# A state-space recurrence issued in another order beside its projections, and small transfers joined

## The chip, the cores and the metric

The kernel runs on one core of one Trainium2 chip. The metric is the device time of one execution in microseconds (us), and lower is better. The engines of the core are TensorE (PE: matmuls; PEld: its weight loads), VectorE (DVE), ScalarE (ACT), GpSimd (POOL) and SyncE (SP). In this kernel every transfer (DMA) is issued on SP.

## The reference

One step of a two-layer decoder trunk of width 1,024, for a prompt of 2,048 tokens and for 8 samples of one token each. The first layer has an RG-LRU and a gated DeltaNet of 8 heads side by side; the second is a complex diagonal state-space model (S5) with 64 groups of 16 channels and 64 complex states per group; a final RMSNorm follows. The second layer, cut to what matters:

```python
def s5_mixer(h, ...):
    u, z = jnp.split(jnp.dot(h, in_w), 2, axis=-1)
    ...
    Bu = einsum("gpc,blgc->lbgp", B_bar, u)
    Bu[0] += A_bar * x0                     # the given state, zero for the prompt
    xs = associative_scan(x[t] = A_bar * x[t-1] + Bu[t])
    y = einsum("gcp,lbgp->blgc", C, xs).real + d * u
    y = gelu(y)
    y = y * sigmoid(y @ glu_w + glu_b)      # the GLU
    y = y * silu(z)                         # the gate path
    return y @ out_w, xs[-1].real, xs[-1].imag
```

## The kernel before, in words

The prompt is worked in two halves of 1,024 tokens; in half 0 the 8 samples ride along as 8 more columns (1,032). Every projection is done in units: 128 output channels by all columns, 8 blocks of the contraction dimension (k = 0 to 7), and three matmuls each, because operands are split into a high and a low part (`in_unit`, L865, its matmul at L876). A unit's results leave PSUM by an `evac` function.

**Background work.** The recurrences run beside the units as generators in lanes (class `Fibers`, L35). After each `BURST` = 1,536 columns of projection matmuls, `pump` lets each lane go on by one step, that is to its next `yield`; `wait(n)` is n steps. `drain` runs a lane to its end with no projection matmul between. A scheduler with priorities then sets each engine's final order, and each engine runs its queue in that order; so the order rows below are read, and not the code's order alone.

**Second layer, per half** (loop at L1838). The first product of the layer gives u (8 units) and z (8 units). For i = 0 to 9 the loop does u-unit i and then z-unit i − 2, so the order is u0 u1 u2 z0 u3 z1 ... u7 z5 z6 z7. After u-unit i its result goes through DRAM (`dU`) into a transposed tile `uc`, the block's lane (`s50` for even i, `s51` for odd) is drained, and the block's generator `s5` is added to it. A z-unit leaves SiLU(z) in `sz`, and one unit later GpSimd multiplies it by the block's result `yg` (L1876). After the loop both lanes are drained, all 8 `yg` are split into high and low parts, and 8 GLU units and 8 output units follow.

**A block, `s5`** (L1702): 128 channels, 8 groups, in two quads of four groups, one after the other. It waits 9 steps and loads a table `MT`. A quad loads its tables `RT`, `ct`, `st`, waits 6 steps, and does four matmuls with `RT` (L1729); VectorE multiplies and adds (`s5t`), 4 steps later (6 in half 0) does four scans, and multiplies and adds again; 14 steps after the scans four pairs of matmuls with `MT` and `O` follow (L1786, L1787), and ScalarE puts the GELU back into `uc`. In half 0 a quad also carries the samples: matmuls at L1740, a transpose at L1749, `s5xa` on VectorE, matmuls at L1776 (`s5uo`), two more steps of waiting. At a block's end `uc` goes through DRAM (`dY`) into `yg`.

**Other parts that the change touches.** Weights come by a `Stream` (L242) that is one unit ahead; in half 0 of a layer ScalarE and GpSimd split them (`wlo`, L234). `final0` (L1815) is the final norm of half 0, 8 blocks: load `xf`, multiply on VectorE (L1834), store; it runs in lane `fn` during half 1's recurrence, every second step. In the first layer `gdn_prep` inverts triangular 16 x 16 blocks of a head: matrix `AT` (L964) goes to DRAM in 8 pieces (`fsd`) and comes back as `fsA` (F), VectorE solves in 15 steps (L1001), the results go to DRAM (`fst`) and come back in 16 pieces as `zt`, `zo` and `U32`, which the DeltaNet's matmuls read (L1053).

Of the kernel before, what the change touches and what calls it, by code (L numbers as in the profile page):

```python
# [2071 lines left out]
```

## Time and profile before

| | |
|---|---|
| time, median of 3 runs | 3163.17 us (3158.49 to 3163.83) |
| the profiled execution's own time | 3162.53 us |
| its span (first to last instruction) | 3160.6 us |
| mean granted TensorE clock | 0.967 of full speed |
| busy: PE, PEld, DVE, ACT, POOL | 2946.8, 2577.6, 2077.0, 1109.6, 689.1 us |
| DMA | 51.0% of 16 engines' time, 404,136 packets, 532.09 MB |
| chain of waits, by engine | PE 57%, DVE 26%, DMA 7%, issue 4% |

A window's row gives the stretch in us from the span's start, its length, and for PE, PEld, DVE, ACT and POOL the busy us (and instructions); then the granted TensorE clock (1.00 is 2.4 GHz, 0.50 is 1.2 GHz), the DMA share and GB/s. The stages are: 100 to 930 the first half of the first layer, 930 to 1170 the end of it with the output projection, 1170 to 2003 its second half; in the second layer 2215 to 2520 the recurrence of half 0, 2520 to 2610 its GLU, 2712 to 2960 the recurrence of half 1, and 3050 to 3160 the last output projection with the final norm. A waits row names the instruction that waited, by engine, tile and line, and what ended the wait. In a timeline row the bracket is the engine's idle time just before, with its releaser. L127 and L115 are helpers that record many VectorE instructions and all DMAs; there the tiles' names tell them apart.

### The profile page before, as it was taken

The page shows a single profiled execution, that of the slowest core. Times are in us where ns is not written, and L with a number is a line of the kernel's source. Part 1 is how long each engine was busy: PE and PEld are TensorE (multiplying, and loading weights), DVE is VectorE, ACT ScalarE, POOL GpSimd, SP SyncE. Part 2 cuts the span into 40 slices and gives each one's busy share as a digit, 9 for nine tenths or more (in the row PEclk, how much of TensorE's full clock was granted, in tenths as well). Part 3 has the DMA queues.
Part 4 walks back from the last instruction along what each step waited for, and adds up shares of the span by engine and source line. Part 5 has one row for each costly group of instructions (what it writes and reads, how often), then busy time and mean ns, then how long its engine had stood idle before and what let it go on. Part 6 is the DMA issues. An engine that isn't in the chain of part 4 may idle for free.

```text
span 3160.6 us, 54048 instructions
## 1 busy us (share of the span) xinstructions
PE 2946.8 (93%) x19958; PEld 2577.6 (82%) x19958; DVE 2077.0 (66%) x5468; ACT 1109.6 (35%) x2023; POOL 689.1 (22%) x672
## 2 busy tenths in 40 slices
PE   5999998999999999999999999999978899989998
PEld 3888888888887777777777777899868899877786
DVE  7896986677894877866756787445655534565524
ACT  3544444444543324433334343412211233110222
POOL 3233433223442323021111111101112222000100
PEclk8999999999999999999999999999989899999999
DMA  6344344443537873444434324555566548587442
GB/s 231 123 134 155 116 160 152 134 143 133 168 125 262 274 227 125 130 128 157 122 129 144 122 88 138 180 182 200 185 218 214 184 144 293 196 298 248 150 134 87
DMA packets 404136, 532.09 MB, mean 168 GB/s; under 512 B 143520, under 2 KB 210592, under 8 KB 403872
## 3 DMA queue, kind: packets, MB, share of 16 engines
q1 hardware_dynamic: 403872, 528.63, 51.0%
q8 instruction: 158, 2.59, 0.3%
q14 instruction: 106, 0.87, 0.1%
HBM read 328.11 MB, written 200.36 MB: 167 GB/s over the span
## 4 chain that ended last, share of the span: by engine, by line
PE 57%; DVE 26%; DMA 7%; issue 4%; ACT 2%; POOL 2%; SPq 2%; DVEq 0%; POOLq 0%; ACTq 0%
PE ps_mm L876 44%; DVE s5t L127 4%; DVE c_v L856 2%; SPq L115 2%; DVE xc L856 1%; DVE fsP L1004 1%; DMA yk<-yd 1%; DVE c_q L856 1%; DVE fsT L1006 1%; PE ps_pre L1787 1%; POOL wlo L234 1%; DVE D L910 1%; PE ps_ch L1139 1%; PE ps_ch L1145 1%; PE ps_pre L1786 1%
## 5 line engine op out<-in xcount | busy, mean ns | idle before, releaser
L876 PE MATMUL ps_mm<-hh,wlo 128*128 128x512 f32 (+2 forms) x2536 | 791.6, 373 | 0.0
L876 PE MATMUL ps_mm<-hh,whi 128*128 128x512 f32 (+2 forms) x2536 | 761.5, 361 | 4.7 <-DVE sz L1872 2.3
L876 PE MATMUL ps_mm<-hl,whi 128*128 128x512 f32 (+2 forms) x2536 | 748.7, 356 | 0.0
L876 PEld LDWEIGHTS ps_mm<-hl,whi 128*128 128x128 f32 x2536 | 480.2, 192 | 44.5 <-issue 0.2
L876 PEld LDWEIGHTS ps_mm<-hh,whi 128*128 128x128 f32 x2536 | 472.3, 192 | 53.5 <-DVE sz L1872 2.7
L876 PEld LDWEIGHTS ps_mm<-hh,wlo 128*128 128x128 f32 x2536 | 449.9, 192 | 35.7 <-issue 7.7
L234 POOL TENSOR_TENSOR wlo<-wraw,whi 128x512 fp32r<-128x512 f32 (+1 forms) x200 | 277.3, 1394 | 664.9 <-ACT whi L233 429.5
L876 PE MATMUL ps_mm<-yl,whi 128*128 128x512 f32 (+2 forms) x640 | 187.9, 356 | 3.0 <-DVE yl L234 3.0
L876 PE MATMUL ps_mm<-yh,whi 128*128 128x512 f32 (+2 forms) x640 | 185.1, 358 | 5.8 <-ACT yh L233 5.8
L876 PE MATMUL ps_mm<-yh,wlo 128*128 128x512 f32 (+2 forms) x640 | 189.8, 359 | 0.0
L233 ACT ACTIVATE whi<-wraw 128x512 fp32r<-128x512 f32 (+1 forms) x200 | 121.9, 618 | 119.5 <-DMA wraw<-in_wo 42.5
L1136 ACT ACTIVATE qs<-ps_ch,geg 128x128 f32<-128x128 f32 x128 | 47.1, 368 | 297.7 <-DVE rr L1133 293.8
L856 DVE SCALAR_TENSOR_TENSOR c_k<-raw,cbw,c_k 128x256 f32<-128x256 f32 x192 | 91.0, 513 | 73.7 <-ACT c_k L893 72.8
L876 PEld LDWEIGHTS ps_mm<-yh,whi 128*128 128x128 f32 x640 | 118.3, 191 | 17.9 <-ACT yh L233 7.3
L876 PEld LDWEIGHTS ps_mm<-yl,whi 128*128 128x128 f32 x640 | 119.9, 191 | 15.6 <-DVE yl L234 4.8
L876 PEld LDWEIGHTS ps_mm<-yh,wlo 128*128 128x128 f32 x640 | 118.3, 191 | 9.8
L892 ACT ACTIVATE raw<-ps_mm 128x384 f32<-128x384 f32 (+1 forms) x160 | 81.6, 513 | 74.4 <-PE ps_mm L876 70.9
L876 PE MATMUL ps_mm<-y2h,whi 128*128 128x384 f32 (+3 forms) x344 | 100.4, 340 | 0.1
L876 PE MATMUL ps_mm<-y2h,wlo 128*128 128x384 f32 (+3 forms) x344 | 99.9, 339 | 0.0
L876 PE MATMUL ps_mm<-y2l,whi 128*128 128x384 f32 (+3 forms) x344 | 99.6, 338 | 0.0
L856 DVE SCALAR_TENSOR_TENSOR c_v<-raw,cbw,c_v 128x256 f32<-128x256 f32 x192 | 95.1, 529 | 4.0 <-ACT c_v L893 3.8
L856 DVE SCALAR_TENSOR_TENSOR xc<-raw,caw,xc 128x256 f32<-128x256 f32 x192 | 94.7, 514 | 4.2 <-ACT xc L893 3.5
(669 smaller groups left out, 5754.2 us busy)
## 6 DMA issues: line engine op xcount, KB each, us to landing
wraw<-in_w SPq DMA_DIRECT2D x128, 256.0 KB, 3.8
whw<-whi SPq DMA_DIRECT2D x128, 256.0 KB, 2.5
wlw<-wlo SPq DMA_DIRECT2D x128, 256.0 KB, 2.4
whi<-whw SPq DMA_DIRECT2D x128, 256.0 KB, 4.4
wlo<-wlw SPq DMA_DIRECT2D x128, 256.0 KB, 4.2
modw<-in_modw SPq DMA_DIRECT2D x48, 512.0 KB, 5.7
yk<-yd SPq DMA_DIRECT2D x32, 512.0 KB, 5.8
xk<-x1d SPq DMA_DIRECT2D x32, 512.0 KB, 5.7
```

Of the source, the lines that this page charges most:

```text
L115: SP.dma_start(out, in_)
L127: return getattr(self.eng, op)(*args, **kw)
L233: a = A.activation(hi, src, AF.Identity)
L234: return a, (lo_eng or V).tensor_tensor(lo, src, f(hi), op=OP.subtract)
L856: V.scalar_tensor_tensor(d, raw[:, a * n + j:a * n + j + n], wt[:, tile_i, j:j + 1], d, op0=OP.mult, op1=OP.add)
L876: PE.matmul(p, w[:, c], x[:, b0:b1], start=(k == 0 and x is hh[k] and w is wh), stop=(k == 7 and w is wl))
L892: A.activation(raw[:, 3 + b0:3 + e], p[:, 0:e - b0], AF.Copy)
L910: V.tensor_scalar(dc[:, c], dc[:, c], tok["gc"][:, c, h:h + 1], 0.0, op0=OP.subtract, op1=OP.min)
L1004: V.tensor_tensor(pr_[:, 0:i, 0:i], Ti[:, 0:i, 0:i].rearrange("p j c -> p c j"), bc(F[:, 0:i, i].unsqueeze(1), s), op=OP.mult)
L1006: V.tensor_reduce(Ti[:, i, 0:i], pr_[:, 0:i, 0:i], axis=AX.X, op=OP.add, negate=True)
L1136: A.activation(qs, p1[:, 1, :], AF.Copy, scale=g["eg"][:, c:c + 1])
L1139: PE.matmul(p2_, U[:, c, :], rr, start=True, stop=True)
```

## The change

In the second layer:

- The units come in another order, `ORDER`: u0 u1 z0 u2 z1 u3 z2 u4 z3 u5 z4 u6 u7 z5 z6 z7. The weights are streamed in the same order.
- The two quads of a block become two generators. The second starts `SPACE` = 16 steps after the first; both go on in one step of the lane.
- A lane is no longer drained in the loop: blocks queue up in it. After the loop only `s50` is drained; `s51` is drained inside the first GLU unit, ahead of its k = 7 (`late`), where the last `yg` is split. For this that unit has all its column blocks in one group.
- `gate()` issues the GpSimd product for every block whose `sz` and `yg` exist.
- The samples' loads and stores are done once per block and no longer once per quad.
- `final0` runs in half 1's output projection, every step.

In the first layer and the tables: `fsd` takes the whole of `AT` in one transfer, with a row pitch such that the diagonal blocks can be read back in one; `zt`, `zo` and a new `zu` are read in one transfer each, and two ScalarE copies with a mask by odd and even blocks make `U32` of `zu`; the tables `cre` and `cim` are loaded in pairs. In all there are 400 DMA issues fewer (2338 to 1938).

```diff
 NS, LOOK, BURST = 8, 2, 1536
+SPACE = 16
...
+ORDER = [(0, 0)] + [x for i in range(5) for x in ((0, i + 1), (1, i))] + [(0, 6), (0, 7)] + [(1, i) for i in (5, 6, 7)]
...
-    def in_unit(hh, hl, blocks, evac, wts=None):
+    def in_unit(hh, hl, blocks, evac, wts=None, late=None):
...
             for k in range(8):
+                if k == 7 and late:
+                    late()
                 wh, wl = wts[k // 4]
...
         fd, ft = fsd[par], fst[par]
-        for b in range(8):
-            dma(fd[:, 16 * b:16 * b + 16, :].rearrange("u j i -> j u i"),
-                AT[16 * b:16 * b + 16, :, 16 * b:16 * b + 16])
+
+        dma(fd[:, 0:128 * 128].rearrange("u (p i) -> p u i", i=128), AT)
         F = TT("fsA", (64, 16, 16))
-        dma(F.rearrange("p j i -> p (j i)"),
-            fd.rearrange("u (b j) i -> (u b) (j i)", b=8))
+        dma(F, fd.rearrange("u x -> (u x)").rearrange("(q x) -> q x", x=16 * 129)[:, 0:16 * 128]
+            .rearrange("q (j i) -> q j i", i=128)[:, :, 0:16])
...
-        zt, zo = TT("zt", (128, 8, 16)), TT("zo", (128, 8, 16))
+        zt, zo, zu = (TT(n, (128, 8, 16)) for n in ("zt", "zo", "zu"))
         U32 = g["U32"] = TT("U32", (128, 8, 32))
-        G.memset(U32, 0.0)
-        fb = [ft[n].rearrange("(u b) (i j) -> b i u j", b=8, i=16) for n in range(2)]
-        for b in range(4):
-            r = 32 * b
-            dma(zt[r:r + 16], fb[0][2 * b])
-            dma(zo[r:r + 16], fb[1][2 * b + 1])
-            dma(U32[r:r + 16, :, 0:16], fb[1][2 * b])
-            dma(U32[r + 16:r + 32, :, 16:32], fb[1][2 * b + 1])
+        fb = [ft[n].rearrange("(u b) (i j) -> (b i) u j", b=8, i=16) for n in range(2)]
+        dma(zu, fb[1])
+        dma(zt, fb[0])
+        dma(zo[0:112], fb[1][16:128])
+        for t in range(2):
+            A.activation(U32[:, :, 16 * t:16 * t + 16], zu, AF.Copy, scale=odd[:, t:t + 1])
...
@@ -1400,11 +1410,8 @@
     for hf in range(2):
         push_half()
     for hf in range(2):
-        for i in range(10):
-            if i < 8:
-                push_unit("w1", i)
-            if i > 1:
-                push_unit("w1", 8 + i - 2)
+        for z, i in ORDER:
+            push_unit("w1", 8 * z + i)
...
@@ -1701,28 +1708,33 @@
 
     def s5(hf, mt, uc, yg, upad):
         Q3 = (128, 4, 128)
+        g8 = slice(mt * 8, mt * 8 + 8)
+        if hf == 0:
+            G8 = (128, 8, 8)
+            xa_, xb_, uo = TT("s5xa", G8), TT("s5xb", G8), TT("s5uo", (16, 8, 8))
+            dma(xa_, I["s5x"][:, g8])
+            dma(xb_, I["s5xs"][:, g8])
+            dma(uo, dUs[mt].rearrange("(c g) b -> c g b", g=8))
+            dma(upad[112:128, :], dUs[mt].rearrange("(c g) b -> c (g b)", g=8))
         yield from wait(9)
         mtm = TA("MT")
         dma(mtm, dMT[mt].rearrange("p g t c -> p (g t c)"))
...
+            dma(cs8, I["cri"][:, g8])
             VH.tensor_scalar(cs8, cs8, nsg[:, 0:1], None, op0=OP.mult)
-        for qd in range(2):
+            VH.tensor_tensor(xa_, xa_, bc(a1[:, 0, g8, None], G8), op=OP.mult)
+            VH.tensor_tensor(xb_, xb_, bc(a1is[:, g8, None], G8), op=OP.mult)
+            VH.tensor_tensor(xa_, xa_, xb_, op=OP.add)
+            VH.tensor_tensor(uo, uo, bc(d16[:, g8, None], (16, 8, 8)), op=OP.mult)
+        def quad(qd):
             cs = slice(qd * 512, qd * 512 + 512)
             g4 = slice(mt * 8 + qd * 4, mt * 8 + qd * 4 + 4)
             tl = {n: TB("s5" + n, FT, Q3) for n in ("RT", "ct", "st")}
             for n, src in (("RT", dRT), ("ct", dC), ("st", dS)):
                 dma(tl[n].rearrange("p g n -> p (g n)"), src[mt][:, cs])
-            if hf == 0:
-                xa_, xb_ = TT("s5xa", (128, 4, 8)), TT("s5xb", (128, 4, 8))
-                dma(xa_, I["s5x"][:, g4, :])
-                dma(xb_[0:64], I["s5x"][64:128, g4, :])
-                dma(xb_[64:128], I["s5x"][0:64, g4, :])
-                uo = TT("s5uo", (16, 4, 8))
-                dma(uo, dUs[mt].rearrange("(c g) b -> c g b", g=8)[:, qd * 4:qd * 4 + 4, :])
+            l4 = slice(qd * 4, qd * 4 + 4)
...
-                VH.tensor_tensor(xa_, xa_, pws[:, :, 0:8], op=OP.add)
-                dma(O["s_s5"][:, g4, :], xa_)
+                VH.tensor_tensor(xa_[:, l4], xa_[:, l4], pws[:, :, 0:8], op=OP.add)
+                if qd == 1:
+                    dma(O["s_s5"][:, g8, :], xa_)
...
-                VH.tensor_tensor(uo, uo, bc(d16[:, g4, None], (16, 4, 8)), op=OP.mult)
-                VH.tensor_tensor(uo, uo, pys[0:16], op=OP.add)
-                AH.activation(uo, uo, AF.Gelu_apprx_tanh)
-                dma(dYs[mt][:, qd * 32:qd * 32 + 32], uo.rearrange("c g b -> c (g b)"))
+                VH.tensor_tensor(uo[:, l4], uo[:, l4], pys[0:16], op=OP.add)
+                if qd == 1:
+                    AH.activation(uo, uo, AF.Gelu_apprx_tanh)
+                    dma(dYs[mt], uo.rearrange("c g b -> c (g b)"))
...
             yield
+
+        quads = [quad(0)]
+        n = 0
+        while quads:
+            if n == SPACE:
+                quads.append(quad(1))
+            quads = [x for x in quads if next(x, x) is not x]
+            n += 1
+            if quads:
+                yield
         dma(dY[hf, mt].rearrange("t (c g) n -> (t c) (g n)", g=8), uc.rearrange("p g n -> p (g n)"))
...
+        gated = []
+
+        def gate():
+            for m in range(8):
+                if m in sz and m in yg and m not in gated:
+                    G.tensor_tensor(sz[m], sz[m], yg[m], op=OP.mult)
+                    gated.append(m)
+
+        for z, i in ORDER:
+            if z == 0:
...
                     dU[hf, i].rearrange("t (c g) n -> (t c) (g n)", g=8))
-                bg.drain(f"s5{i % 2}")
                 if hf == 0:
-                    upad = upads[i % 2]
                     dma(dUs[i], ut[:, HT:W1])
-                    dma(upad[112:128, :], dUs[i].rearrange("(c g) b -> c (g b)", g=8))
                 bg.add(s5(hf, i, uc, yg, upads[i % 2]), f"s5{i % 2}")
-                if hf == 1 and i == 1:
-                    bg.drain("fin")
-                    bg.add(final0(), "fn", 2)
-            m = i - 2
-            if m >= 0:
-                sz[m] = TA("sz1", FT, (128, n))
+            else:
+                sz[i] = TA("sz1", FT, (128, n))
...
 
                 in_unit(hh, hl, blocks, evac_s)
-                if m > 0:
-                    G.tensor_tensor(sz[m - 1], sz[m - 1], yg[m - 1], op=OP.mult)
-        bg.drain("s50", "s51")
-        G.tensor_tensor(sz[7], sz[7], yg[7], op=OP.mult)
+                gate()
+        bg.drain("s50")
         yh, yl = {}, {}
-        for m in range(8):
-            yh[m], yl[m] = TA("ygh", FR, (128, n)), TA("ygl", FR, (128, n))
-            split(yh[m], yl[m], yg.pop(m))
+
+        def glu_in(*ms):
+            for m in ms:
+                yh[m], yl[m] = TA("ygh", FR, (128, n)), TA("ygl", FR, (128, n))
+                split(yh[m], yl[m], yg[m])
+
+        def last_in():
+            bg.drain("s51")
+            glu_in(7)
+            gate()
+
+        gate()
+        glu_in(*range(7))
         y2h, y2l = {}, {}
...
                 A.activation(h_, z, AF.Identity, scale=0.25)
                 V.scalar_tensor_tensor(l_, z, 0.25, f(h_), op0=OP.mult, op1=OP.subtract)
 
-            in_unit(yh, yl, blocks, evac_g)
+            if m == 0:
+                in_unit(yh, yl, (tuple(blk for grp in blocks for blk in grp),), evac_g, late=last_in)
+            else:
+                in_unit(yh, yl, blocks, evac_g)
         x2 = {}
         sq = Squares()
         hh, hl = {}, {}
         ahead = prep1(1, hh, hl) if hf == 0 else iter(())
         bg.drain("fin")
+        if hf == 1:
+            bg.add(final0(), "fn")
         x1 = {}
 
```

How the instructions stand. TensorE in half 0 of the second layer, before: the first rows of one burst (`ps_pre` and `ps_ch` are PSUM tiles of the recurrence, no row of the projection's `ps_mm` is among them).

```order
L1749 MATMUL ps_ch<-ident,s5us 128x128
L1729 MATMUL ps_pre<-uc,s5RT 128x128 x4
L1740 MATMUL ps_ch<-s5RT,upad_25131 32x128 x4
L1786 MATMUL ps_pre<-uc,MT 128x128
L1749 MATMUL ps_ch<-ident,s5us 128x128
L1776 MATMUL ps_ch<-s5xa,cs_25746 16x8 x4
L1786 MATMUL ps_pre<-uc,MT 128x128
L1776 MATMUL ps_ch<-s5xa,cs_26141 16x8 x4
L1787 MATMUL ps_pre<-s5t_26165,s5O_26271 128x128
L1786 MATMUL ps_pre<-uc,MT 128x128
L1787 MATMUL ps_pre<-s5t_26165,s5O_26271 128x128
```

After, at the end of one quad and the beginning of the next one's sample work:

```order
L1796 MATMUL ps_pre<-uc,MT 128x128
L1797 MATMUL ps_pre<-s5t_25086,s5O_25168 128x128
L1796 MATMUL ps_pre<-uc,MT 128x128
L1797 MATMUL ps_pre<-s5t_25086,s5O_25168 128x128
L1758 MATMUL ps_ch<-ident,s5us 128x128 x2
L889 MATMUL ps_mm<-hh,wlo 128x384
L889 MATMUL ps_mm<-hh,whi 128x384
L889 MATMUL ps_mm<-hl,whi 128x384
L889 MATMUL ps_mm<-hh,wlo 128x384
```

Here rows of `ps_mm` (L889 is the projection) follow right behind the transposes of two quads at L1758; in the burst before, rows of several quads stand among each other, and none of the projection.

VectorE in half 0, before: two quads with numbers 26165/26166 and 26224/26225.

```order
L127 SCALAR_TENSOR_TENSOR s5t_26166<-rho_145,l_25126,s5t_26165 128x128
L127 TENSOR_TENSOR s5t_26224<-s5t_26224,s5t_26225 128x512
L127 SCALAR_TENSOR_TENSOR s5t_26166<-rho_145,l_25126,s5t_26165 128x128 x3
L127 COPY s5ct<-l_25126 128x4
L127 TENSOR_TENSOR s5xb<-s5xb,l_25126 128x32
L127 COPY l_25126<-s5t_26166 128x4
L127 TENSOR_TENSOR s5ct<-s5ct,s5t_26166 128x4x127
L127 TENSOR_TENSOR s5t_26165<-s5st,s5t_26166 64x4x127 x2
L127 TENSOR_TENSOR s5xa<-s5xa,a_146 128x32
L127 SCALAR_TENSOR_TENSOR s5t_26225<-rho_145,l_25126,s5t_26224 128x128
L127 TENSOR_TENSOR s5t_26165<-s5t_26165,s5ct 128x512
```

After: one quad, 25728/25729.

```order
L132 TENSOR_TENSOR s5t_25728<-ps_pre,s5ct 128x512
L132 TENSOR_TENSOR s5t_25729<-ps_pre,s5st 64x512 x2
L132 COPY s5ct<-l_24828 128x4
L132 TENSOR_TENSOR s5t_25728<-s5t_25728,s5t_25729 128x512
L132 TENSOR_TENSOR s5xa<-s5xa,ps_ch 128x32
L132 SCALAR_TENSOR_TENSOR s5t_25729<-rho_145,l_24828,s5t_25728 128x128 x4
L132 COPY l_24828<-s5t_25729 128x4
L132 TENSOR_TENSOR s5ct<-s5ct,s5t_25729 128x4x127
L132 TENSOR_TENSOR s5t_25728<-s5st,s5t_25729 64x4x127 x2
L132 TENSOR_TENSOR s5t_25728<-s5t_25728,s5ct 128x512
L132 COPY l_24828<-s5ct 128x4
L132 TENSOR_SCALAR l_24828<-s5st,nsg 128x4
```

The rows of two quads alternated and each quad's last sum came behind a part of the other's scans; now a quad's rows follow each other.

SP in the first layer, before: what brings a head's solve back from DRAM.

```order
L115 DMA fst_172<-fsT 64x256
L115 DMA fst_172<-fsU 64x256
L115 DMA dMT<-zero 128x512 x2
L115 DMA zt<-fst_172 16x8x16
L115 DMA zo<-fst_172 16x8x16
L115 DMA U_3094<-fst_172 16x8x16 x2
L115 DMA zt<-fst_172 16x8x16
L115 DMA zo<-fst_172 16x8x16
L115 DMA U_3094<-fst_172 16x8x16 x2
```

After:

```order
L120 DMA fst_172<-fsT 64x256
L120 DMA fst_172<-fsU 64x256
L120 DMA dMT<-zero 128x512
L120 DMA whw_26_1_3175<-whi 128x512
L120 DMA wlw_26_1_3176<-wlo 128x512
L120 DMA zu<-fst_172 128x8x16
L120 DMA zt<-fst_172 128x8x16
L120 DMA zo<-fst_172 112x8x16
L120 DMA db<-in_s5d 128x128
```

The rows for zt, zo and U (three more such rounds follow in before) are now three, with `zu` first, and a weight store stands ahead of them.

## Rows read from the trace of the kernel before

**Rows 1.** windows by stage: length, busy by engine, clock, DMA share, GB/s

```profile
100.00:930.00 830.00, 768.48 (x6210) 719.41 (x6209) 665.82 (x1954) 392.38 (x777) 288.39 (x277) 0.97 0.44 140
930.00:1170.00 240.00, 233.92 (x1288) 189.45 (x1287) 166.26 (x361) 81.34 (x127) 79.14 (x78) 0.97 0.79 264
1170.00:2003.00 833.00, 811.01 (x5639) 643.09 (x5637) 599.83 (x1806) 344.38 (x611) 149.34 (x158) 0.99 0.40 124
2215.00:2520.00 305.00, 262.24 (x1827) 248.07 (x1827) 170.54 (x421) 60.59 (x140) 59.59 (x53) 0.92 0.64 203
2520.00:2610.00 90.00, 88.62 (x564) 88.15 (x563) 35.70 (x51) 33.14 (x64) 22.46 (x15) 1.00 0.42 145
2712.00:2960.00 248.00, 224.69 (x1130) 186.58 (x1128) 150.91 (x279) 29.97 (x53) 19.19 (x23) 0.97 0.73 245
3050.00:3160.00 110.00, 95.70 (x483) 80.63 (x481) 41.53 (x93) 24.57 (x35) 6.44 (x6) 0.93 0.31 106
```

**Rows 2.** TensorE's waits, half 0 of the second layer: us in total, times, longest

```profile
PE ps_ch L1776 <- DVE s5xa L127: 22.0, 6, 7.8
PE ps_pre L1729 <- DMA s5RT<-dRT: 4.2, 3, 3.2
```

**Rows 3.** TensorE's waits, half 1 of the second layer

```profile
PE ps_pre L1787 <- DVE s5t L127: 16.2, 8, 4.5
```

**Rows 4.** timeline of TensorE in half 0: start, length, instruction, idle before

```profile
2316.39 1.13 PE L1729 MATMUL ps_pre<-uc,s5RT 128*128 128x128 f32 x8 [1.94 <-issue]
2328.65 0.38 PE L1776 MATMUL ps_ch<-s5xa,cs 128*16 128x8 f32 x8 [7.83 <-DVE s5xa L127]
2333.35 0.67 PE L876 MATMUL ps_mm<-hh,whi 128*128 128x384 f32 x1
```

**Rows 5.** windows of 10 us from within that burst on

```profile
2320.00:2330.00 10.00, 0.87 (x10) 0.58 (x10) 9.91 (x25) 0.63 (x1) 2.78 (x4) 0.61 0.55 180
2330.00:2340.00 10.00, 8.77 (x44) 8.80 (x45) 5.27 (x13) 2.47 (x6) 4.89 (x3) 0.71 0.55 169
```

**Rows 6.** timeline of VectorE in half 1, one quad's first and last instruction

```profile
2861.02 0.69 DVE L127 TENSOR_TENSOR s5t<-ps_pre,s5ct 128x512 f32<-128x512 f32 x1 [11.17 <-PE ps_pre L1729]
2868.40 0.68 DVE L127 TENSOR_TENSOR s5t<-s5t,s5ct 128x512 f32<-128x512 f32 x1
```

**Rows 7.** DMA issues: out<-in, KB each, median us from issue to landing

```profile
zd<-zbs SPq DMA_DIRECT2D x16, 512.0 KB, 4.1
s5RT<-dRT SPq DMA_DIRECT2D x32, 256.0 KB, 4.4
dY<-uc SPq DMA_DIRECT2D x16, 512.0 KB, 2.9
xf<-x2d SPq DMA_DIRECT2D x8, 512.0 KB, 6.4
fsd<-AT SPq DMA_DIRECT2D x128, 8.0 KB, 1.5
fsA<-fsd SPq DMA_DIRECT2D x16, 64.0 KB, 2.7
zt<-fst SPq DMA_DIRECT2D x64, 8.0 KB, 2.5
```

**Rows 8.** VectorE by line, 2520 to 3160 us: busy and mean, idle before

```profile
L1834 DVE SCALAR_TENSOR_TENSOR xf<-xf,fnw,rows 128x1024 f32<-128x1024 f32 x8 | 11.8, 1474 | 15.6 <-DMA xf<-x2d 15.5
```

**Rows 9.** SP's issues of `fsd`: ns min/median/max

```profile
L115 SPq DMA_DIRECT2D fsd<-AT x128: 302/428/1528, 121.4 to 1955.3; - x128
```

**Rows 10.** TensorE's waits in the first layer

```profile
PE ps_pre L1053 <- DMA zt<-fst: 3.2, 2, 1.7
```

**Rows 11.** VectorE's waits in the first layer

```profile
DVE fsP L1004 <- DMA fsA<-fsd: 5.8, 5, 1.7
```

**Rows 12.** GpSimd by line, half 0 of the second layer

```profile
L234 POOL TENSOR_TENSOR wlo<-wraw,whi 128x512 fp32r<-128x512 f32 x30 | 41.0, 1373 | 72.3 <-ACT whi L233 47.9 <-DVE s5t L127 7.5 <-DMA wraw<-in_w 6.2
L1876 POOL TENSOR_TENSOR sz<-sz,yg 128x1032 f32<-128x1032 f32 x7 | 16.8, 2402 | 27.7 <-DVE sz L1872 20.4 <-DMA wlw<-wlo 4.5 <-DVE s5uo L127 2.8
```

More of the change, by code (lines that the diff above doesn't have):

```diff
@@ L632, in s5_tables @@
         C8 = (128, 8, 16)
-        for off, x, y in ((624, "cre", "cim"), (752, "cim", "cre")):
-            dma(gp[0:64, off:off + 128].rearrange("p (g c) -> p g c", c=16), I[x][:, g8])
-            dma(gp[64:128, off:off + 128].rearrange("p (g c) -> p g c", c=16), I[y][:, g8])
+        for off, x in ((624, "cri"), (752, "cir")):
+            dma(gp[:, off:off + 128].rearrange("p (g c) -> p g c", c=16), I[x][:, g8])
         zero = TB("zero")
@@ L731, in hybrid_step @@
     gcd = [D(f"gcd{i}", (8, 8, 128)) for i in range(2)]
-    fsd = [D(f"fsd{i}", (8, 128, 16)) for i in range(2)]
+    fsd = [D(f"fsd{i}", (8, 128 * 129)) for i in range(2)]
     fst = [D(f"fst{i}", (2, 64, 256)) for i in range(2)]
+    oi, odd = TT("oddi", (128, 1), I32), K("odd", (128, 2))
+    G.iota(oi, pattern=[[0, 1]], base=0, channel_multiplier=1)
+    V.tensor_scalar(oi, oi, 4, 1, op0=OP.logical_shift_right, op1=OP.bitwise_and)
+    V.tensor_copy(odd[:, 1:2], oi)
+    V.tensor_scalar(odd[:, 0:1], odd[:, 1:2], -1.0, 1.0, op0=OP.mult, op1=OP.add)
     ss0 = {1: K("ss0", (128, 8))}
@@ L1775, in s5 @@
                 for j in range(4):
-                    PE.matmul(pys[0:16, j, :], cs8[:, qd * 4 + j, :], xa_[:, j, :],
+                    PE.matmul(pys[0:16, j, :], cs8[:, qd * 4 + j, :], xa_[:, qd * 4 + j, :],
                               start=True, stop=True)
-                VH.tensor_tensor(uo, uo, bc(d16[:, g4, None], (16, 4, 8)), op=OP.mult)
-                VH.tensor_tensor(uo, uo, pys[0:16], op=OP.add)
-                AH.activation(uo, uo, AF.Gelu_apprx_tanh)
-                dma(dYs[mt][:, qd * 32:qd * 32 + 32], uo.rearrange("c g b -> c (g b)"))
+                VH.tensor_tensor(uo[:, l4], uo[:, l4], pys[0:16], op=OP.add)
+                if qd == 1:
+                    AH.activation(uo, uo, AF.Gelu_apprx_tanh)
+                    dma(dYs[mt], uo.rearrange("c g b -> c (g b)"))
             yield from wait(8)
@@ L1841, in hybrid_step @@
         yg, sz = {}, {}
-        for i in range(10):
-            if i < 8:
+        gated = []
[6 more added lines that the diff above has]
+            if z == 0:
                 ut = TA("ut", FT, (128, n))
@@ L1871, in evac_s @@
                     A.activation(t, p, AF.Tanh, scale=0.5)
-                    V.scalar_tensor_tensor(sz[m][:, b0:b1], t, 1.0, p, op0=OP.add, op1=OP.mult)
+                    V.scalar_tensor_tensor(sz[i][:, b0:b1], t, 1.0, p, op0=OP.add, op1=OP.mult)
                 in_unit(hh, hl, blocks, evac_s)
-                if m > 0:
-                    G.tensor_tensor(sz[m - 1], sz[m - 1], yg[m - 1], op=OP.mult)
-        bg.drain("s50", "s51")
-        G.tensor_tensor(sz[7], sz[7], yg[7], op=OP.mult)
+                gate()
+        bg.drain("s50")
         yh, yl = {}, {}
-        for m in range(8):
-            yh[m], yl[m] = TA("ygh", FR, (128, n)), TA("ygl", FR, (128, n))
-            split(yh[m], yl[m], yg.pop(m))
+        def glu_in(*ms):
[8 more added lines that the diff above has]
+        glu_in(*range(7))
         y2h, y2l = {}, {}
@@ L2008, in layouts @@
         "s5x": np.concatenate([state_s5_re[0], state_s5_im[0]], axis=2).transpose(2, 1, 0),
+        "s5xs": np.concatenate([state_s5_im[0], state_s5_re[0]], axis=2).transpose(2, 1, 0),
         "w1": c_in_w[0].reshape(8, 128, 16, 8, 16).transpose(2, 1, 0, 4, 3).reshape(16, 128, 1024),
@@ L2017, in layouts @@
         "bim": s5_b_im[0].transpose(1, 0, 2),
-        "cre": s5_c_re[0].transpose(2, 0, 1),
-        "cim": s5_c_im[0].transpose(2, 0, 1),
+        "cri": np.concatenate([s5_c_re[0], s5_c_im[0]], axis=2).transpose(2, 0, 1),
+        "cir": np.concatenate([s5_c_im[0], s5_c_re[0]], axis=2).transpose(2, 0, 1),
         "s5d": s5_d[0].reshape(8, 8, 16),
```

5 lines of the change are left out of this document (removed).

## The prediction

> **What bounds the kernel now.** I read the table of windows first, one window per stage. TensorE is busy 811.01 of 833 us in the first layer's second half and 88.62 of 90 in the GLU, but 262.24 of 305 and 224.69 of 248 in the two stages of the second layer's recurrence [rows 1]. So the kernel is bound by TensorE nearly everywhere, and these two stages are where it is not. What they lose: half 0 has 305 − 262.24 = 42.8 us idle, and a granted clock of 0.92, which costs about (1 − 0.92) × 305 = 24.4 us; together 67. Half 1 has 248 − 224.69 = 23.3 us idle and (1 − 0.97) × 248 = 7.4 of clock; together 31. In all 98 us are there to be had.
>
> The waits say who ends the idle time: in half 0 TensorE waits 22.0 us in 6 pieces at L1776 for VectorE's `s5xa` and 4.2 us for the table `s5RT` [rows 2]; in half 1 it waits 16.2 us in 8 pieces at L1787 for VectorE's `s5t` [rows 3]. VectorE is not full (170.54 of 305 us), so this is a matter of order and not of its rate. The timeline shows how: from 2316.39 to 2333.35 TensorE has nothing in its queue but the pieces of two groups of four (quads, below) whose chains VectorE works through one after the other, and it stands still for 7.83 us at once [rows 4]. It is the place at which the program empties a lane: the rest of a block is issued there with no projection matmul between. The two windows of 10 us from 2320 on have a granted clock of 0.61 and 0.71, between the levels of 1.2 and 2.4 GHz, with TensorE busy 0.87 us in the first [rows 5]; so an idle burst is paid for twice.
>
> **The recurrence, part by part.** One quad's chain on VectorE, from its first product at 2861.02 to the end of its last sum at 2868.40 + 0.68, is 8.1 us in half 1 [rows 6]. In half 0 everything on VectorE, sample work and gates included, is 170.54 / 16 quads = 10.7 us per quad. The cover is counted in lane steps. A step is 1,536 columns, a unit has 1,024 or 1,032 columns times 24, so 16 steps; eight GLU units take about 90 us [rows 1], 11.1 us each, so a step is 0.69 us. The code has 18 steps between a quad's first matmul and its output matmuls in half 1 (2 + 2 + 6 + 8) and 20 in half 0: 12.4 and 13.8 us, more than 8.1 and 10.7. One quad alone is therefore hidden before and after. Two quads whose chains meet need 16.2 or more, and that is not.
>
> Before, a block takes 9 + 2 × 27 = 63 steps in half 0, and lane 0's second block comes two units, 32 steps, after its first, lane 1's second 48 after its first: the drain must issue the rest in one burst. After, a block's second quad begins 16 steps (11.1 us) behind the first, so a block takes 9 + 16 + 27 = 52 steps; the new block order starts lane 0's blocks 48 and then 64 steps apart and lane 1's 64, and nothing is drained between. The order of after shows a quad's first matmuls every 13 us or so in half 0, its sample product some 9.5 us behind them and its output matmuls apart from both, each with projection matmuls between; one early bunch of two quads is left there, and a few pairs in half 1. The last block starts after 13 units, 208 steps, and ends some 4 to 6 steps into the first GLU unit, which begins at 256 and whose k = 7 comes 14 steps later. Then dY (2.9 us to landing [rows 7]), the load of yg and the split of the last unit must fit in some 8 us of matmuls: 0 here, with 4 us per half if it does not.
>
> What is left: the neighbouring stages of the same kind of work lose 7.4% + 3% (100 to 930 us) and 2.6% + 1% (1170 to 2003 us) [rows 1]. On some 240 us that is 25 or 9 in half 0, on 217 us 23 or 8 in half 1. I take 20 in half 0, nearer the upper one because of the early bunch, and 8 in half 1, whose order is the more regular. Gain: 67 − 20 = 47 and 31 − 8 = 23, together 70. The bounds are none of it and all 98.
>
> Late next are the tables: a quad's RT is loaded 6 steps (4.1 us) before its matmuls and lands after 4.4 us in the median [rows 7], yet TensorE waited for it only 4.2 us in all in half 0 [rows 2], as it is usually issued earlier. The stage's transfers do not change, except that final0's go: 0.64 × 305 = 195 us of DMA time in 240 is 0.81. The stage from 930 to 1170 runs at 0.79 with TensorE busy 233.92 of 240 [rows 1], so I put no loss on it.
>
> **final0.** Eight loads and eight stores of 512 KB and 8 products of 1.47 us on VectorE (11.8 us, with 15.5 us of idle behind the loads [rows 8]) leave half 1's recurrence and go to its output projection, where TensorE has 95.70 of 110 us and DMA 0.31 [rows 1]. They run every step now, so a load has 4 steps, 2.8 us, before VectorE reaches its product, and lands after 6.4 [rows 7]: VectorE can stand (6.4 − 2.8) × 8 = 29 us with the output units' sums queued behind. TensorE has four PSUM buffers there, two units' worth and so some 20 us of cover for each stand of 3.6 us. I take 0; the bound is −7 (freed waits in half 1) to +29.
>
> **Fewer DMAs in the first layer.** Per head 25 small issues become 5. Before, 8 `fsd` issues take 8 × 0.428 = 3.4 us on SP, land 1.5 us later, and `fsA`, issued in about the same 0.43, lands after 2.7 [rows 7, 9]: 8.0 us from AT to F. After, one write of 512 KB takes 0.43 + 2.9 (as dY<-uc) to 4.1 (as zd<-zbs), and F is read in 1,024 pieces of 64 bytes, which lies between 2.7 (as now) and twice that: with its own 0.43 6.5 to 10.4 us, so −1.5 to +2.4 per head. Behind the solve, 16 issues (6.8 us) and a landing of 2.5 [rows 7] become 3 issues and a landing of perhaps 3: about 5 us earlier per head. But little waits for these: TensorE 3.2 us for zt in all [rows 10], VectorE 5.8 us for fsA [rows 11]. The upper gain is their sum, 9; the upper loss 16 × 2.4 = 38, if every F lands later and nothing covers it. I take −3. The 32 added copies on ScalarE and the memsets that leave GpSimd lie beside engines that are not the bound; 0. The sample loads once per block take SP issues out of half 0; that is in its 47.
>
> **Sum.** 70 + 3 = 73 off the profiled execution's 3162.5 us (span 3160.6 and 1.9 around it): 3089.5, forecast 3090. That execution is 0.6 us under the median of the runs, 3163.17, which changes nothing.
>
> **The rivals.**
> 1. Half of it only: what TensorE stops waiting for on VectorE it waits for elsewhere, on tables that land after their 4.1 us, or at the bunch that is left. For it: RT's 4.4 us and a DMA share of about 0.8; against it the stage at 0.79 that runs full. Half of 70 and nothing in layer 1: 3162.5 − 35 = 3127.
> 2. All of it: the recurrence runs as the GLU stage does, at 98% and full clock, and the waits for zt and fsA go too: 3162.5 − 98 − 9 = 3055. For it, the regular distances in the order; against it, no stage of mixed work here loses less than 3.6%.
> 3. The pieces of F come late, 2.4 us per head on a path that nothing covers: 3090 + 3 + 38 = 3131. For it, VectorE already waits for fsA in 5 of 16 heads [rows 11]; against it, only 5.8 us in all, with a solve that is issued among other heads' work. The Trainium skill speaks for it: "DMA: Bandwidth & Descriptors", section Specifications, asks for transfers of at least 512 bytes for full rate, and says smaller ones are done as read-modify-write. The trace bears that out in part at most: zt's 64-byte pieces land after 2.5 us with 8 KB, fsA's 64 KB in 1 KB pieces after 2.7.
> 4. Slower than before, by GpSimd's queue. `gate()` puts a product in as soon as a yg is known to the program, before its transfer has landed (dY 2.9 us, then yg), and GpSimd runs in order: the weight splits of half 0 (1.37 us each, 30 of them) stand behind it [rows 12]. Weights are made one unit ahead, 11.1 us, so it decides from a product's wait of more than 11.1 us. If each of 7 products held the splits for a unit longer than that, 7 × 11.1 = 78 us, and the clock after each wait some (0.39 + 0.29) × 10 = 6.8 more by [rows 5], 47 in all, it would be 3090 + 78 + 47 = 3215. Against it, a yg takes some 7 us from its first store, and the products waited 20.4 us in all before [rows 12] with no wait of TensorE for a weight in [rows 2].
>
> **How the numbers follow.** Forecast 0.52 (own range 3070 to 3108), half of it 0.19, all of it 0.14, late F 0.08, GpSimd's queue 0.04, and 0.03 for no change, where the two recurrences keep their losses because the chains meet as before. A measurement of this kernel tells about 0.2%, 6 us, from no change. The first four cases are faster; with something for milder forms of the slower ones: faster 0.90, same 0.04, slower 0.06. The range runs from the all-of-it case at 3055 to just past the late F case, 3135.
>
> **What would show it.** Right: the recurrence of half 0 takes some 258 us and of half 1 some 225, TensorE's waits for `s5xa` and `s5t` fall under 8 us together, and no window of 10 us there has a clock under 0.8. The final norm's products stand among the output units with no wait of TensorE on them. In the first layer both halves keep their lengths within some 5 us, AT to F takes 7 to 9 us, and TensorE waits for no zt. Wrong: waits for `s5RT` or `s5O` of more than 10 us (rival 1), waits of VectorE for fsA of more than 20 (rival 3), or waits of TensorE for wlo (rival 4).

## The result, and the profile after

The changed kernel takes 3080.52 us (median of 4 runs, 3076.75 to 3083.2) against 3163.5 before: the ratio is 0.9737, 95% interval 0.9714 to 0.976, so 83 us less (76 to 90). Forecast were 3090 us, 73 less. The profiled execution took 3082.49 us, span 3080.8.

Where the 79.8 us between the two spans lie is read from the first and last starts of TensorE's matmuls by tile, which bound the stages: `yh` is the first layer's output projection, `hh` the first product, `ygh` the GLU and `y2h` the output projection of the second.

| from | to | before | after | less |
|---|---|---|---|---|
| start | first `yh` | 941.1 | 923.1 | 18.0 |
| first `yh` | last `yh` (second half of layer one) | 1269.6 | 1269.2 | 0.4 |
| last `yh` | first `ygh` (half 0, recurrence) | 305.8 | 266.1 | 39.7 |
| first `ygh` | first `y2h` (half 0, GLU) | 93.9 | 102.4 | −8.5 |
| first `y2h` | first `hh` of half 1 | 91.1 | 92.1 | −1.0 |
| first `hh` of half 1 | first `ygh` (half 1, recurrence) | 257.3 | 227.1 | 30.2 |
| first `ygh` | first `y2h` (half 1, GLU) | 91.5 | 91.5 | 0.0 |
| first `y2h` | end | 110.3 | 109.3 | 1.0 |

The table of windows of after has these stages in its rows (columns as in [rows 1]): the first layer's first half, then half 0's recurrence and GLU, and half 1's recurrence.

```profile
100.00:923.00 823.00, 765.55 (x6304) 718.08 (x6302) 669.25 (x1970) 403.07 (x802) 292.59 (x274) 0.99 0.48 151
2194.00:2460.00 266.00, 249.64 (x1797) 236.57 (x1796) 178.80 (x388) 55.82 (x128) 60.52 (x51) 0.96 0.70 228
2460.00:2561.00 101.00, 97.56 (x611) 96.90 (x612) 42.85 (x61) 35.74 (x69) 25.86 (x17) 0.97 0.43 147
2650.00:2885.00 235.00, 231.61 (x1215) 195.09 (x1215) 140.45 (x263) 35.92 (x60) 19.09 (x23) 1.00 0.70 230
```

Half 1 is idle 3.4 us of 235 at full clock, where [rows 1] had 23.3 idle and 0.97. Half 0 still loses 266 − 249.64 = 16.4 us, and 0.04 × 266 = 10.6 by the clock. TensorE's waits of after, half 0 and then half 1, answer to [rows 2, 3]:

```profile
PE ps_pre L1741 <- DMA s5RT<-dRT: 7.8, 4, 3.2
PE ps_mm L889 <- ACT ut L1875: 6.4, 1, 6.4
PE ps_mm L889 <- DVE ygl L239: 3.6, 2, 2.0
PE ps_ch L1786 <- DVE s5xa L132: 0.4, 1, 0.4
```

```profile
PE ps_pre L1741 <- DVE s5t L132: 1.1, 1, 1.1
PE ps_pre L1796 <- DVE s5t L132: 0.7, 1, 0.7
```

The 22.0 us for `s5xa` became 0.4 and the 16.2 for `s5t` 1.8. New is a wait of 6.4 us at an ordinary projection matmul for ScalarE's `ut`. The timelines of TensorE, ScalarE and VectorE show its chain:

```profile
2240.63 0.56 PE L1786 MATMUL ps_ch<-s5xa,cs 128*16 128x8 f32 x16
2247.63 0.69 PE L889 MATMUL ps_mm<-hh,whi 128*128 128x384 f32 x1 [6.45 <-ACT ut L1875]
```

```profile
2246.95 0.26 ACT L132 ACTIVATE s5uo<-s5uo 16x64 f32<-16x64 f32 x1 [3.82 <-DVE s5uo L132]
2247.11 0.46 ACT L1875 ACTIVATE ut<-ps_mm 128x384 f32<-128x384 f32 x1
```

```profile
2234.63 0.69 DVE L132 TENSOR_TENSOR s5t<-ps_pre,s5ct 128x512 f32<-128x512 f32 x1 [0.28 <-PE ps_pre L1741]
2246.75 0.17 DVE L132 TENSOR_TENSOR s5uo<-s5uo,ps_ch 16x32 f32<-16x32 f32 x1
```

This is the early bunch that the order showed. Two quads are on VectorE at once, the samples' `s5uo` comes behind most of their rows, ScalarE stands in its queue at the GELU of it, `ut` (which copies a projection's result out of PSUM) stands behind that, and TensorE waits for the PSUM buffer that `ut` frees: the wait passes through three queues, each worked off in order. The window of 10 us there, 2240 to 2250, has TensorE busy 3.55 us and a clock of 0.67. A second profile of the changed kernel (e12 below) has the same wait of 6.4 us.

In the first layer the DMA rows answer to [rows 7]:

```profile
fsd<-AT SPq DMA_DIRECT2D x16, 512.0 KB, 3.4
fsA<-fsd SPq DMA_DIRECT2D x16, 64.0 KB, 3.0
zt<-fst SPq DMA_DIRECT2D x16, 64.0 KB, 3.9
```

VectorE's waits for fsA went from [rows 11] to the first row below, TensorE's for zt from [rows 10] to the second:

```profile
DVE fsP L1016 <- DMA fsA<-fsd: 3.0, 2, 1.9
PE ps_pre L1063 <- DMA zt<-fst: 0.5, 1, 0.5
```

### The profile page after: what moved, and what is told of

Same layout as the page of the kernel before. It is cut to its first block, busy times and chain, and to the rows that moved or that the text cites. A ratio compares the mean times of both kernels' runs of the same rounds, so it can differ in the third digit from the quotient of the medians.

```text
span 3080.8 us, 53370 instructions
## 1 busy us (share of the span) xinstructions
PE 2912.8 (95%) x19958; PEld 2552.6 (83%) x19958; DVE 2080.2 (68%) x5439; ACT 1113.8 (36%) x2046; POOL 684.9 (22%) x657
## 5 line engine op out<-in xcount | busy, mean ns | idle before, releaser
L889 PE MATMUL ps_mm<-hh,wlo 128*128 128x512 f32 (+2 forms) x2536 | 783.1, 371 | 0.0
L889 PE MATMUL ps_mm<-hh,whi 128*128 128x512 f32 (+2 forms) x2536 | 749.3, 358 | 7.8 <-ACT ut L1875 6.4
L889 PE MATMUL ps_mm<-hl,whi 128*128 128x512 f32 (+2 forms) x2536 | 736.3, 353 | 0.0
L889 PEld LDWEIGHTS ps_mm<-hh,whi 128*128 128x128 f32 x2536 | 466.5, 190 | 58.1 <-ACT ut L1875 6.5
L889 PEld LDWEIGHTS ps_mm<-hl,whi 128*128 128x128 f32 x2536 | 475.4, 190 | 44.5
L889 PEld LDWEIGHTS ps_mm<-hh,wlo 128*128 128x128 f32 x2536 | 442.9, 191 | 34.6 <-issue 7.7
L889 PE MATMUL ps_mm<-yh,whi 128*128 128x512 f32 (+2 forms) x640 | 185.9, 359 | 10.3 <-ACT yh L238 8.5
L889 PE MATMUL ps_mm<-yh,wlo 128*128 128x512 f32 (+2 forms) x640 | 190.9, 361 | 0.0
L889 PE MATMUL ps_mm<-yl,whi 128*128 128x512 f32 (+2 forms) x640 | 187.4, 357 | 0.4 <-DVE yl L239 0.4
L238 ACT ACTIVATE whi<-wraw 128x512 fp32r<-128x512 f32 (+1 forms) x200 | 121.4, 617 | 101.2 <-DMA wraw<-in_wo 39.8
L889 PEld LDWEIGHTS ps_mm<-yh,whi 128*128 128x128 f32 x640 | 119.0, 192 | 22.9 <-ACT yh L238 9.8
L889 PEld LDWEIGHTS ps_mm<-yl,whi 128*128 128x128 f32 x640 | 120.4, 192 | 12.2 <-DVE yl L239 1.0
L889 PEld LDWEIGHTS ps_mm<-yh,wlo 128*128 128x128 f32 x640 | 118.8, 192 | 9.8
L889 PE MATMUL ps_mm<-y2h,whi 128*128 128x384 f32 (+3 forms) x344 | 100.0, 338 | 0.5 <-DVE x L132 0.3
L889 PE MATMUL ps_mm<-y2h,wlo 128*128 128x384 f32 (+3 forms) x344 | 99.1, 337 | 0.0
L889 PE MATMUL ps_mm<-y2l,whi 128*128 128x384 f32 (+3 forms) x344 | 99.1, 337 | 0.0
L889 PE MATMUL ps_mm<-ygl,whi 128*128 128x384 f32 (+2 forms) x320 | 92.5, 355 | 5.4 <-DVE ygl L239 5.4
```

The lines of the kernel that those rows point to most:

```text
L238: a = A.activation(hi, src, AF.Identity)
L889: PE.matmul(p, w[:, c], x[:, b0:b1], start=(k == 0 and x is hh[k] and w is wh), stop=(k == 7 and w is wl))
```

## The experiments

Each was timed beside the kernel before on one chip. A ratio is this time over that of the kernel before, with its 95% interval. Executions of one kernel lie up to 1.2% apart (the kernel before beside e12 to e15: 3154.31 to 3191.16 us), so the interval is ±0.2 to 0.4%, 5 to 12 us. "Against after" is the ratio's distance from 0.9737 times 3163 us; as 0.9737 itself is known to ±7 us, such a difference is known to some ±9 to 14 us. Those of e3, e5, e11 and e14 are clear of that, the others are not. The stages of the profiled executions (bounded as in the table) show where the time went, but from one execution each: e7's is the slowest of its six (3098.48 us, median 3080.14), e4's the fastest of its six (3073.71, median 3083.72).

**The first layer's transfers alone, and undone.**

```diff
 # e1: before with this; e2: after without
-        for b in range(8):
-            dma(fd[:, 16 * b:16 * b + 16, :].rearrange("u j i -> j u i"),
-                AT[16 * b:16 * b + 16, :, 16 * b:16 * b + 16])
+        dma(fd[:, 0:128 * 128].rearrange("u (p i) -> p u i", i=128), AT)
...
+        dma(zu, fb[1])
+        dma(zt, fb[0])
+        dma(zo[0:112], fb[1][16:128])
```

> The kernel before with the first layer's DMA change alone (AT written in one transfer, zu/zt/zo in three, U32 from zu by ScalarE). The first layer came out 18 us shorter with the whole change. Theory A: that is these transfers, 18 us, so about 3145. Rival B: they are worth the 3 us of the prediction and the 18 come from elsewhere (the tables' loads, or how the order fell), so 3160, within 0.2% of before. Rival C: the 64-byte pieces cost, 3170 or more.

> The changed kernel with the first layer's transfers as before. Theory A: the first layer gets its 18 us back, 3098. Rival B: 3083, within 0.2% of the changed kernel. In both, the second layer keeps its gain of 60.

Measured: e1 3146.09 us, ratio 0.9935 (0.991 to 0.996), 21 us less than before (13 to 28); e2 3089.3, ratio 0.976 (0.9733 to 0.9787), 7 more than after. The second layer had in e1 the lengths of before (half 0's two stages 400.3, half 1's 348.1) and in e2 those of after (363.6 and 320.9). So by e1 the transfers are worth more than 3 us. How much of 18: the start to first `yh` is 941.1 and 932.4 in the two kernels with the old transfers, 929.7 in e1, and 923.0 to 937.1, mean 929.1, in the eleven profiles of the changed kernel and its variants with the new ones, the same instructions there each time. By these profiles about 8 us of the 18 are the transfers and the rest the luck of one execution, though 932.4 lies inside the range of the eleven. The timed runs do not agree on it: 13 to 28 by e1, and 7, known to ±11, by e2. Their share stays open between some 8 and 20 us.

**The distance of the quads, the drain, and both.**

```diff
 # e3 (second quad when the first has ended), and e14
-            if n == SPACE:
-                quads.append(quad(1))
             quads = [x for x in quads if next(x, x) is not x]
-            n += 1
+            n += not quads
+            if n == 1 and not quads:
+                quads.append(quad(1))
 # e5, and e14
+                bg.drain(f"s5{i % 2}")
                 bg.add(s5(hf, i, uc, yg, upads[i % 2]), f"s5{i % 2}")
```

> The changed kernel with the two quads of a block one after the other again (no distance of 16 steps); new order, no drain, late last block kept. Theory of spacing: a block takes 63 steps and the two lanes' quads come 5 steps apart in seven pairs per half, whose chains then need 16 to 20 us against a cover of 12 to 14; about +30, 3110. Rival: it was only the drain that cost, so within 6 us of 3080.

> The changed kernel with the lane drained again in each iteration of the loop. By counting steps a block now takes 52 steps and the next block of its lane comes after 48 only once (block 2 in lane 0) and after 48 in lane 1's last, so at most some 4 steps are issued in a burst twice per half: theory: +0 to +6, 3080 to 3086. Rival: a drain costs as it did before, +20 or more.

> The changed kernel with both undone: quads one after the other and the lane drained in each iteration. Alone, they cost 19 and 13 us. Theory: one makes the other worse, as a block of 63 steps must be drained where a block of 52 hardly is; 40 to 55 us, most of what the second layer gained, 3120 to 3135. Rival: they add up, 32, 3112, and the rest of the gain lies in the samples' work and the norm.

Measured: e3 3099.44 us, ratio 0.9789 (0.9762 to 0.9816), 16 against after; e5 3094.0, 0.978 (0.9763 to 0.9797), 14; e14 3117.71, 0.9844 (0.9807 to 0.9881), 34. They about add up, as the rival for e14 had it. The measured e3 lies between its theory and its rival, and e5 above the 0 to 6 expected of it. Half 0's two stages take 368.5 us in after, 380.1 in e3, 372.7 in e5 and 391.4 in e14, of 399.7 before; half 1's 318.6, 325.6, 322.6 and 325.9, of 348.8. So the two edits carry most of half 0's gain (391.4 − 368.5 = 23 of 31; alone 12 and 4) and 7 of 30 in half 1.

The bursts themselves can be counted in TensorE's rows, as stretches of more than 4 us from the start of one projection matmul to the next. Before has 6 of them in half 0 and 6 in half 1 (62.5 and 39.1 us in all), after 3 and 1 (17.1 and 4.6), and e14 has 6 and 2 (39.2 and 9.4). So the two edits bring the bursts back in half 0 and hardly in half 1. Nor do they bring back the waits of [rows 2, 3], 22.0 us for `s5xa` and 16.2 for `s5t`. TensorE's waits of e14, half 0 and then half 1:

```profile
PE ps_pre L1797 <- DMA s5O<-dO: 6.7, 2, 4.7
PE ps_pre L1797 <- DVE s5uo L132: 6.4, 1, 6.4
PE ps_ch L1786 <- DVE s5xa L132: 1.0, 2, 0.6
```

```profile
PE ps_pre L1797 <- DVE s5t L132: 1.6, 2, 0.9
```

What a few drained steps cost in e5: TensorE's waits there, and VectorE's timeline before the largest.

```profile
PE ps_mm L889 <- DVE sz L1894: 11.3, 1, 11.3
```

```profile
2420.67 0.68 DVE L132 TENSOR_TENSOR s5t<-ps_pre,s5ct 128x512 f32<-128x512 f32 x1
2437.39 0.17 DVE L132 TENSOR_TENSOR s5uo<-s5uo,ps_ch 16x32 f32<-16x32 f32 x1
2437.49 1.80 DVE L1894 SCALAR_TENSOR_TENSOR sz<-th,ps_mm 128x384 f32<-128x384 f32 x4
```

Two quads meet, VectorE is on them for 16.8 us, and four evacuations of a z-unit stand behind. TensorE waits 11.3 us for a PSUM buffer, and not for a quad. I had counted the drained steps and not what stands behind the chains.

**The order of the units.**

```diff
-ORDER = [(0, 0)] + [x for i in range(5) for x in ((0, i + 1), (1, i))] + [(0, 6), (0, 7)] + [(1, i) for i in (5, 6, 7)]
+ORDER = [(0, 0), (0, 1)] + [x for i in range(6) for x in ((0, i + 2), (1, i))] + [(1, 6), (1, 7)]
```

> The changed kernel with the old order of units (u0 u1 u2 z0 u3 ...); distance of 16 steps, no drain and late last block kept. By counting steps two pairs of quads of the two lanes still meet exactly (steps 41 and 93 of a half) as two do in the changed kernel (41 and 217): theory: 0 to +8, 3080 to 3088. Rival: the order carries the gain, +20 or more, 3100.

Measured: 3083.72 us, ratio 0.9739 (0.9712 to 0.9766), 1 against after. Half 0 takes 360.0 and half 1 316.5, no longer than after. With the quads at a distance and no drain, the order is worth nothing that was measured. What it is worth beside quads in sequence and a drain was not run, and e14 has the new order: there lane 0's second block starts 48 steps after its first and not 32, so that its drain has less to issue in one burst. The old order together with both edits of e14 is therefore a rival that stands untested for what e14 does not bring back.

**The late last block.**

```diff
-        bg.drain("s50")
+        bg.drain("s50", "s51")
...
-        glu_in(*range(7))
+        glu_in(*range(8))
```

> The changed kernel with both lanes drained ahead of the GLU and all eight splits there (no late last block). Theory: some 6 steps of the last block, its way through DRAM (about 7 us) and its split stand open at the end of each half, about 12 us each with the clock after it, so +24, 3105. Rival: the tail was hidden anyway or the late block costs as much in the GLU (8 us more there in half 0), 0 to +6.

Measured: 3080.14 us, ratio 0.9748 (0.9723 to 0.9774), 3 against after. Half 0's recurrence takes 273.0 and its GLU 94.6, together 367.6; with the late block 266.1 and 102.4, 368.5. What the recurrence gains by it the GLU gives back; in half 1 it is worth some 5 us by the profiles (324.1 to 318.6). My theory for it falls.

**The final norm moved back.**

```diff
+                if hf == 1 and i == 1:
+                    bg.drain("fin")
+                    bg.add(final0(), "fn", 2)
...
-        if hf == 1:
-            bg.add(final0(), "fn")
```

> The changed kernel with half 0's final norm back in half 1's recurrence. Theory: VectorE stands behind eight loads there again (15.5 us before) and the quads queued behind it come late; +4 to +12, 3085 to 3092. Rival of the prediction: nothing, within 6 us of 3080.

Measured: 3086.43 us, ratio 0.9763 (0.9744 to 0.9781), 8 against after, which is within the noise; half 1 takes 322.9 against 318.6, and VectorE stands behind the eight loads for 17.1 us. In after the products stand behind their loads for 6.2 us and nothing on TensorE waits for them:

```profile
L1854 DVE SCALAR_TENSOR_TENSOR xf<-xf,fnw,rows 128x1024 f32<-128x1024 f32 x8 | 10.2, 1281 | 9.3 <-DMA xf<-x2d 6.2 <-ACT rows L418 3.1
```

**The quads that still meet.** By steps, two pairs of the lanes' quads begin together in after.

```diff
-SPACE = 16
+SPACE = 14
+HOLD = {1: 12, 2: 8, 3: 4, 7: 8}
...
-        yield from wait(9)
+        yield from wait(9 + HOLD.get(mt, 0))
```

> The changed kernel with a distance of 14 steps and blocks 1, 2, 3 and 7 held back by 12, 8, 4 and 8 steps, so that no two quads of the two lanes begin in the same step (in the changed kernel those of steps 41 and 217 do). Theory: the 27 us that half 0's recurrence still loses are for a good part these meetings (a wait of 6.45 us at one of them, with the clock after it); -8 to -15, 3065 to 3072. Rival: late tables (7.8 us of waits in half 0) or the DMA share set what is left: within 6 us of 3080.

Measured: 3094.63 us, ratio 0.9785 (0.9768 to 0.9801), 15 against after: slower. The wait for `ut` is gone as meant, but in half 0 there are others:

```profile
PE ps_pre L1742 <- DMA s5RT<-dRT: 7.1, 3, 4.3
PE ps_mm L890 <- DVE sz L1894: 4.8, 1, 4.8
PE ps_mm L890 <- ACT ygh L239: 4.3, 1, 4.3
```

The last block ends later, as the edit holds it back by 8 steps: its last output matmuls start 16.7 us after the first GLU matmul in half 0 (12.5 in after) and 13.0 us after it in half 1 (0.5 us ahead of it in after). Both GLU stages grow (106.3 from 102.4, 96.9 from 91.5). The theory that the meetings alone are what is left falls.

**The changed kernel again, the samples per quad, and their stores later.**

```diff
 # e13: as before the change
+                dma(xa_, I["s5x"][:, g4, :])
+                dma(xb_[0:64], I["s5x"][64:128, g4, :])
+                dma(xb_[64:128], I["s5x"][0:64, g4, :])
...
 # e15
-                if qd == 1:
-                    dma(O["s_s5"][:, g8, :], xa_)
...
+        if hf == 0:
+            A.activation(uo, uo, AF.Gelu_apprx_tanh)
+            dma(dYs[mt], uo.rearrange("c g b -> c (g b)"))
+            dma(O["s_s5"][:, g8, :], xa_)
         dma(dY[hf, mt].rearrange("t (c g) n -> (t c) (g n)", g=8), uc.rearrange("p g n -> p (g n)"))
```

> The changed kernel once more, as it is, so that the next three have it beside them on the same chip: 3080 again, 3074 to 3087. If it lies at 3090, differences under 10 us between the earlier runs and it tell nothing.

> The changed kernel with the samples' loads, products and stores once per quad again (distance of 16, no drain, order, late block kept). Theory: a part of half 0's gain is these, since VectorE stood 13.1 us behind loads of s5xb in the kernel before and TensorE 22.0 us behind s5xa; half 0 gets 8 to 15 us back, 3090 to 3095. Rival (the prediction): the bursts were the cause and the sample loads worth nothing, within 6 us of the changed kernel.

> The changed kernel with the samples' last work of a block (GELU, stores of dYs and of the state) issued at the block's end. In the changed kernel SP waited 19.1 us in half 0 for s5xa before the state's store, with the tables of the next quads queued behind it, and TensorE 7.8 us for s5RT. Theory: these 7.8 go with some clock behind them, -6 to -10 against the changed kernel. Rival: SP then waits for the GELU in the same place, or another wait takes over: within 4 us.

Measured: again 3080.61 us, ratio 0.9731 (0.9693 to 0.9769). The samples per quad: 3089.24, 0.9748 (0.9715 to 0.9781); half 0's two stages take 367.9 against 362.9 and 368.5 in the two profiles of the changed kernel, so no more than 5 us are shown, less than the theory's 8 to 15. The stores later: 3077.4 us, 0.9702 (0.9668 to 0.9736), the fastest that was run. By the ratios it lies 9 us under the changed kernel beside it, by the medians 3, and the intervals overlap, so that the timed runs do not decide between theory and rival. Half 0 takes 356.2, 6.7 less than the faster of those two profiles. SP's timeline of after shows the wait that was aimed at:

```profile
2395.45 0.41 SPq L120 DMA_DIRECT2D l<-dUs  x1
2400.31 0.36 SPq L120 DMA_DIRECT2D out_s_s<-s5xa  x1
...
2402.18 0.38 SPq L120 DMA_DIRECT2D s5RT<-dRT  x1
```

SP stands 4.5 us before the store of a state that VectorE has not done, with the next quad's table behind it. In half 0 such stands sum to the first row below in after and to the second in e15, and TensorE's wait for the table to the third in e15, from 7.8:

```profile
SPq L120 <- DVE s5xa L132: 19.1, 8, 4.4
```

```profile
SPq L120 <- DVE s5xa L132: 4.5, 4, 2.1
```

```profile
PE ps_pre L1741 <- DMA s5RT<-dRT: 1.1, 2, 0.9
```

## Why the prediction was right, point by point

- **Where the gain is.** Right: the two recurrences, by waits of TensorE on VectorE's chains and the clock after them. They and their GLUs give 31.2 + 30.2 = 61.4 of 79.8 us; forecast 70. That quads in sequence and drained lanes cost most of half 0's share is shown (e14: 23 of 31 us, with six bursts again). Which part of the change took away the very waits that the prediction read, for `s5xa` and `s5t`, is not shown: in no variant of the changed kernel does TensorE wait more than 4.0 us for `s5xa` in half 0 (e4) or more than 1.9 for `s5t` in half 1 (e5).
- **Half 0, 47 forecast, 31.2 measured (36.8 in the second profile).** Mis-sized. The term of 20 us for what is left was too small: the stage keeps 27, and the GLU, for which I put 0, takes 8.5 more. The term for the tail failed: the late block was to end 4 to 6 steps (2.8 to 4.2 us) into the GLU and to cost nothing. Its last output matmuls start 12.5 us after the first GLU matmul, and what it takes out of the recurrence is paid in the GLU (e7). The count of steps also had lane 1's blocks 64 steps apart, where the last comes after 48, under a block's 52. The tables came late as named there, and not for their landing but for SP's queue: a store that waits stands ahead of them (e15). Nor did I price ScalarE's queue behind the samples' GELU, where the early bunch now ends.
- **Half 1, 23 forecast, 30.2 measured.** The loss of 31 went nearly whole; I had left 8. The cause is only partly shown: by the profiles quads and drain undone give back 7, the norm 4, the late block 5, the order alone nothing. Some 14 us of 30 come from edits together that I did not undo together, the old order with quads in sequence and a drain above all, or from none that I took; this stays open.
- **The first layer, 3 forecast, 18.4 measured.** Mis-sized too, on the other side of half 0's error, so that the sum came out nearer than its terms; that was luck. Some 8 us are the transfers by the profiles, near the bound of 9 that I gave and did not take, and more by e1. In the two profiles most of the 18 us are clock: TensorE's idle time from the 100th us to the first `yh` is 62.5 us before and 57.4 after, but its clock is 0.97 and 0.99. After one wait of 3.0 us for VectorE in the kernel before (in the window from 280) the next window runs at 0.50, the level of 1.2 GHz:

```profile
280.00:290.00 10.00, 7.00 (x72) 6.07 (x71) 1.29 (x4) 3.45 (x8) 2.75 (x3) 0.89 0.57 194
290.00:300.00 10.00, 10.00 (x67) 9.32 (x63) 4.31 (x14) 3.57 (x9) 0.02 (x1) 0.50 0.09 34
```

- **F in 64-byte pieces.** For the first head it is 6.6 us from the issue of `fsd` at 122.08 to the first solve step at 128.69, at the lower end of 6.5 to 10.4 (before, by the same reading, 121.4 to 133.39, 12.0 us with VectorE's other rows between, where I had reckoned 8.0); the read lands after 3.0 us against 2.7. The upper bound, twice 2.7, stood on no row. Rival 3 is refuted here. The Trainium skill's rule in "DMA: Bandwidth & Descriptors", section Specifications, that transfers under 512 bytes miss the full rate, cost little at this size: this transfer of 1,024 pieces of 64 bytes took 0.3 us more than one of 64 pieces of 1 KB. `zt`, which now comes in 1,024 such pieces too, lands after 3.9 us, where I had put 3; TensorE waits for it 0.5 us in all.
- **final0.** Right: no wait of TensorE in its new place, 6.2 us of VectorE's behind the loads where up to 29 were feared, and 4 us gained in half 1 by the profiles (e6; 8 by the timed runs, within the noise), towards the −7 end.
- **GpSimd's queue.** A product did wait for its yg, 18.6 us in 4 pieces, the longest 7.1, as worked out; this is under the 11.1 us of cover, and TensorE waited for no weight:

```profile
POOL sz L1867 <- DMA yg<-dY: 18.6, 4, 7.1
```

- **The signs named beforehand.** `s5xa` and `s5t` together 2.2 us, under 8: right. Recurrences of 258 and 225: 266.1 and 227.1. No window under a clock of 0.8: wrong in half 0 (0.67 from 2240 on, 0.71 from 2340 on). Waits for `s5RT` or `s5O` under 10: right, 7.8. Both halves of the first layer within 5 us: wrong, the first is 18 shorter. AT to F in 7 to 9 us: 6.6 where it was read. No wait of TensorE for zt: nearly, 0.5 us once. Waits of VectorE for fsA under 20: right, 3.0.
